# Cached keys and values of the dilation-16 heads: products on GpSimd in float32 and sums on VectorE instead of products on TensorE

## The chip, the cores and the metric

The kernel runs on one core of one Trainium2 chip. Its engines are called as the profile calls them: PE (TensorE, matrix products; its weight loads are PEld), DVE (VectorE), ACT (ScalarE), POOL (GpSimd) and SP (SyncE, which here only starts transfers). The metric is the time of one execution in microseconds (us) on the device; smaller is better.

## The reference

One inference step of a small decoder for 256 prompt tokens and 8 samples of 8 new tokens (T = 320 columns in all): a convolution layer, an MLP, an attention layer, an MLP, a norm. The change lies in the attention layer. It has 8 head slots, and each has three groups of keys: (window, dilation) = (128, 1), (512, 4), (2048, 16). For the new tokens of a sample the scores and the sums over cached keys are

```python
idx = n_past + jnp.arange(S)[:, None] - dilation * jnp.arange(n_keys)[None, :]
kg = k_cat[:, idx_c]
vg = v_cat[:, idx_c]
s = jnp.einsum('bshe,bsnhe->bhsn', q, kg, preferred_element_type=jnp.float32)
...
o = jnp.einsum('bhsn,bsnhe->bshe', p.astype(vg.dtype), vg,
               preferred_element_type=jnp.float32)
```

and the three groups are merged under one softmax. With dilation 16 and 8 new tokens no two tokens of a sample share a cached key: token s of a sample reads the 128 cached positions that are s modulo 16. So the scores of this third group are, for every token, its own 128 keys of 128 elements times its own query, and its output is its own 128 values weighted with its own row of the softmax. All inputs are float32.

## The kernel before

Every large product is done in three passes of a reduced float32 format. `load` brings 1024 KB of weights or of cached keys or values into a ring of 4 tiles `raw`; `split` makes of each half a leading part `wh` on ACT (line 122) and a rest `wl` on DVE (line 123), with rings of 4; PE then multiplies `wh` with the leading part of the other operand, `wh` with its rest, and `wl` with its leading part (lines 142 to 144, function `mm3`).

The attention layer is a list of steps that `Stream.run` writes out in PE's order, by hand: a step has a part for PE (`pe_`), a part for the other engines that comes after the next step (`post`), and possibly a half of a loaded chunk, which is split three halves ahead of its step. `qkv_steps(h)` gives the nine products of head h (36 quarters of 12 instructions on PE), `side(h)` the attention of head h; `merge` lays the side steps of head h-1 among the quarters of head h, by weights. The last head's side steps lie among `wo_steps`, the first 7 eighths of the output product; the eighth head's share (`wob`) comes behind.

For the cached part, `qk` multiplies each sample's queries, laid out as a block-diagonal operand `qpad`, with that sample's cached keys: 512 columns to an instruction, all 8 tokens of a sample against all its keys, and a mask (line 730) leaves to each token its own. Seven chunks of keys to a head, of which `k = 3..6` (four) are the dilation-16 group. `pv` does the same for 13 tiles of values, of which eight are that group's: lines 734 and 735 are the products of the keys, line 796 that of the values. POOL does nothing in this layer but start the 48 transfers that write out new keys and values (line 881), and 15 additions of the norm at its end (line 211).

Of the kernel before, what the change touches and what calls it, by code (L numbers as in the profile page):

```python
# [32 lines left out]
SEQ = 256  # L33
# [15 lines left out]
NKEY = 1664  # L49
# [21 lines left out]
B_MP = B_MS + NKEY  # L71
# [5 lines left out]
def decoder_step(ctx: ExitStack, tc: tile.TileContext, I, O):  # L77
# [38 lines left out]
    def split(raw, u0, units):  # L116
        """the units from u0 as float32r: the leading part, and the rest"""
# [39 lines left out]
    def rsqrt(out, v, after=None, temps=None):  # L157
        """out = v ** -0.5, with a Newton step"""
# [11 lines left out]
    def tokens(acc, n, eps):  # L170
        """(column sums of acc / n + eps) ** -0.5 on every partition, by way of tokens on partitions"""
# [24 lines left out]
    class Norm:  # L196
        """RMSNorm of x: its gain on the way into the next product, 1/rms on the way out"""
# [27 lines left out]
    def weave(a, b):  # L225
        """runs the steps of two lists in step with one another"""
# [10 lines left out]
    if True:  # L237
# [23 lines left out]
        with tc.tile_pool(name="conv", bufs=1) as conv:  # L261
# [27 lines left out]
            def glu_steps(f):  # L289
                """products, gate and windows of block f"""  # L290
# [49 lines left out]
            def tap_steps(fs):  # L340
                """the depthwise convolution of blocks fs: taps on VectorE (summed in PSUM), GpSimd and, for the last
                block, TensorE; then the sums for the LayerNorm"""
# [23 lines left out]
                def pool_taps(i):  # L366
                    # the share of GpSimd's taps that goes with VectorE's tap i
# [109 lines left out]
    def four(src, ps4, hi, lo, norm):  # L477
        """the products of four blocks together, along the contraction"""
# [45 lines left out]
    tmps[0].__exit__(None, None, None)  # L524
    tmp = None
    with tc.tile_pool(name="attn", bufs=1) as ap:
        oo = big.tile([128, 2, H, T], F32R, name="ah")
        oh, ol = oo[:, 0], oo[:, 1]
        zz = big.tile([128, 3 * 1024 + 13 * 128], F32R, name="al")
        qpad = zz[:, :3072].rearrange("p (g b c) -> p g b c", g=3, b=NB)  # L530
        pt = zz[:, 3072:].rearrange("p (t c) -> p t c", t=13)
        dve.tensor_scalar(zz[:, :3072].rearrange("p (a b) -> p a b", b=128),
                          ones[:, None, :].to_broadcast([128, 24, 128]), 0.0, None, op0=OP.mult)
# [10 lines left out]
        class Stream:  # L544
            """Steps in the order of TensorE's program. The weights' and caches' halves are split ahead of their step,
            and what follows a step on the other engines comes after the next step."""
# [9 lines left out]
            def run(self):  # L556
# [16 lines left out]
                for pe_, post, c, p in self.todo:  # L573
# [7 lines left out]
                    if pe_ is not None:  # L581
                        pe_()
# [6 lines left out]
        class Late:  # L589
            """a chunk that is loaded and split when told"""  # L590
# [24 lines left out]
        def side(h):  # L615
            """attention of head h: steps (quarters of a product of the next head that belong after it, step)"""
            E = {}
            L = []

            def step(w, pe_, post=None, chunk=None, part=0):  # L620
                L.append((w, (pe_, post, chunk, part)))

            def v_t(g):
# [13 lines left out]
                step(.3, go, post)  # L637

            def q_fill():
                for g in range(G):  # L640
# [4 lines left out]
            def new_s():  # L645
# [11 lines left out]
                step(.3, go, post)  # L657

            def p_s(i):
                """scores and softmax of the prompt's query block i"""  # L660
# [26 lines left out]
                step(.3, go, post)  # L687

            def p_t(i, c0):
# [7 lines left out]
                step(.3, go, post)  # L697

            def p_o(i):
# [11 lines left out]
                step(.3, go, post)  # L711

            C0 = {0: (0, 512), 2: (512, 128), 3: (640, 512), 5: (1152, 512)}

            def qk(k):
# [363 lines left out]
```

## Time and profile before

| | before |
|---|---|
| median of 3 runs | 3123.1 us (3121.42 to 3123.53) |
| span of the profiled execution | 3120.8 us |
| PE busy | 3046.0 us, 98% of the span |
| DVE busy | 1837.4 us, 59% |
| ACT busy | 1456.2 us, 47% |
| POOL busy | 253.0 us, 8% |

The table comes from one execution taken by the hardware profiler. Its span runs from the first to the last instruction; the time of a run is some 2 us longer. Busy times are those in which an engine has at least one instruction under way. PE works on several at once, so the mean of one PE instruction is longer than the distance between two of them, and the distance is what counts.

### The profile page before, as it was taken

What the parts mean: (1) busy time and instruction counts of PE and PEld (TensorE: products, weight loads), DVE (VectorE), ACT (ScalarE), POOL (GpSimd) and SP (SyncE); (2) the same over time, 40 slices, a digit from 0 to 9 for tenths busy, and PEclk for the clock granted to TensorE, in tenths of its full rate; (3) what the DMA queues carried; (4) which work ended last, traced back from release to release, by engine and by line L of the source; (5) the groups of instructions that cost most, each with busy time, mean ns of one, the idle gap of its engine ahead of it and who ended that gap; (6) DMA issues with size and microseconds to landing.
All of it is one profiled execution on the core that took longest, in us unless ns stands there. A gap on an engine that the chain in (4) does not pass through costs nothing. (4 is left out here: it accounts for less than half of the span.)

```text
span 3120.8 us, 48229 instructions
## 1 busy us (share of the span) xinstructions
PE 3046.0 (98%) x20160; PEld 2972.0 (95%) x20160; DVE 1837.4 (59%) x2360; ACT 1456.2 (47%) x2006; POOL 253.0 (8%) x261
## 2 busy tenths in 40 slices
PE   7998899999999999999999999999999999999998
PEld 6997899999999999999999999998999999999998
DVE  8998754444444444557777777778744444444444
ACT  7877644334334234435555555555532332433442
POOL 3776200000000000000000000000100000000000
PEclk9999999999999999999999999999999999999999
DMA  5443244444444444446666766676444444444442
GB/s 200 138 153 118 103 149 152 150 149 149 149 149 149 149 150 150 152 166 232 241 237 240 264 230 250 239 250 243 148 151 152 153 151 150 149 149 149 149 149 88
DMA packets 80571, 533.41 MB, mean 171 GB/s; under 512 B 11744, under 2 KB 12000, under 8 KB 19808
## 3 DMA queue, kind: packets, MB, share of 16 engines
q1 hardware_dynamic: 74304, 518.14, 47.9%
q0 software_dynamic: 2448, 8.62, 0.7%
q8 instruction: 158, 2.59, 0.3%
q10 hardware_dynamic: 3600, 3.57, 0.3%
q14 instruction: 61, 0.50, 0.0%
HBM read 517.59 MB, written 12.70 MB: 170 GB/s over the span
## 5 line engine op out<-in xcount | busy, mean ns | idle before, releaser
L123 DVE TENSOR_TENSOR wl<-raw,wh 128x1024 fp32r<-128x1024 f32 (+1 forms) x978 | 1200.9, 1236 | 826.4 <-ACT wh L122 825.4
L122 ACT ACTIVATE wh<-raw 128x1024 fp32r<-128x1024 f32 (+1 forms) x978 | 1019.8, 1055 | 1422.0 <-PE mm L143 1196.5
L142 PE MATMUL mm<-bh,wh 128*128 128x320 f32 x3200 | 990.6, 310 | 10.0 <-ACT wh L122 9.2
L143 PE MATMUL mm<-bl,wh 128*128 128x320 f32 x3200 | 986.1, 308 | 0.8 <-DVE bl L153 0.8
L144 PE MATMUL mm<-bh,wl 128*128 128x320 f32 x3200 | 985.3, 308 | 1.2 <-DVE wl L123 1.2
L142 PE MATMUL mm<-ah,wh 128*128 128x320 f32 x2896 | 895.8, 310 | 29.7 <-ACT wh L122 12.9
L144 PE MATMUL mm<-ah,wl 128*128 128x320 f32 x2896 | 894.0, 309 | 0.1
L143 PE MATMUL mm<-al,wh 128*128 128x320 f32 x2768 | 854.9, 309 | 8.2 <-DVE al L153 4.2
L142 PEld LDWEIGHTS mm<-bh,wh 128*128 128x128 f32 x3200 | 600.7, 188 | 17.4 <-ACT wh L122 9.2
L143 PEld LDWEIGHTS mm<-bl,wh 128*128 128x128 f32 x3200 | 600.8, 188 | 8.9 <-DVE bl L153 2.3
L144 PEld LDWEIGHTS mm<-bh,wl 128*128 128x128 f32 x3200 | 600.5, 188 | 2.0 <-DVE wl L123 2.0
L142 PEld LDWEIGHTS mm<-ah,wh 128*128 128x128 f32 x2896 | 544.5, 188 | 36.6 <-ACT wh L122 15.0
L144 PEld LDWEIGHTS mm<-ah,wl 128*128 128x128 f32 x2896 | 544.7, 188 | 1.2 <-DVE wl L123 0.3
L143 PEld LDWEIGHTS mm<-al,wh 128*128 128x128 f32 x2768 | 520.5, 188 | 11.2 <-DVE al L153 5.5
L374 POOL TENSOR_TENSOR pacc<-pacc,prod 128x320 f32<-128x320 f32 x168 | 180.8, 1111 | 75.5 <-ACT prod L373 74.6
L510 DVE TENSOR_TENSOR x<-x,mm 128x320 f32<-128x320 f32 x128 | 62.4, 488 | 177.4 <-PE mm L144 177.4
L505 DVE SCALAR_TENSOR_TENSOR sg<-mm,r 128x320 f32<-128x320 f32 x126 | 61.8, 492 | 162.4 <-PE mm L144 162.1
L384 DVE SCALAR_TENSOR_TENSOR s<-bl,wdw,s 128x320 f32<-128x320 f32 x272 | 130.0, 545 | 0.1
L373 ACT ACTIVATE prod<-bl,wdw 128x320 f32<-128x320 f32 x168 | 91.0, 577 | 27.7 <-POOL pacc L374 27.3
L734 PE MATMUL s<-wh,al 128*128 128x512 f32 (+1 forms) x256 | 96.1, 387 | 0.0
L735 PE MATMUL s<-wl,al 128*128 128x512 f32 (+1 forms) x256 | 90.8, 366 | 0.0
L535 POOL DMA_DIRECT2D cb<-cb x1 | 0.7, 712 | 1011.8 <-DVE acc L211 1011.8
(191 smaller groups left out, 1608.5 us busy)
## 6 DMA issues: line engine op xcount, KB each, us to landing
raw<-w SPq DMA_DIRECT2D x252, 1024.0 KB, 5.0
raw<-qkv SPq DMA_DIRECT2D x72, 1024.0 KB, 5.2
raw<-k SPq DMA_DIRECT2D x48, 1024.0 KB, 5.4
raw<-v SPq DMA_DIRECT2D x48, 1024.0 KB, 5.5
raw<-pw SPq DMA_DIRECT2D x32, 1024.0 KB, 5.1
raw<-pw2b SPq DMA_DIRECT2D x12, 1024.0 KB, 4.9
raw<-woa SPq DMA_DIRECT2D x8, 896.0 KB, 4.9
raw<-pw2a SPq DMA_DIRECT2D x4, 1024.0 KB, 4.9
```

The costliest lines, as they stand in the source:

```text
L122: act.activation(wh[:, :n], r, AF.Copy)
L123: dve.tensor_sub(wl[:, :n], r, wh[:, :n])
L142: pe.matmul(ps, wh, xh, start=start, stop=False)
L143: pe.matmul(ps, wh, xl, start=False, stop=False)
L144: pe.matmul(ps, wl, xh, start=False, stop=stop)
L373: act.activation(seg(pr_), win(f, k), AF.Copy, scale=dw(f, k))
L374: pool.tensor_add(pa, pa, pr_)
L384: dve.scalar_tensor_tensor(a, win(f, k), dw(f, k), a, op0=OP.mult, op1=OP.add)
L505: dve.scalar_tensor_tensor(t, ps, 0.0, norm.r, op0=OP.max, op1=OP.mult)
L510: dve.tensor_add(x[:, ob], x[:, ob], ps)
L734: pe.matmul(ps[:, :n], qpad[:, g, b0 + j], wh[:, j * n:j * n + n], start=False, stop=False)
L735: pe.matmul(ps[:, :n], qpad[:, g, b0 + j], wl[:, j * n:j * n + n], start=False, stop=(done and j == nb - 1))
```

## The change

The 32 products of keys and the 32 of values that belong to the dilation-16 group leave PE, in each head, and so do the splits of their 8 chunks, the mask's two products and the rows of the mask. In their place each head has 16 pieces, 8 of keys and 8 of values, one to a sample (`piece`): SP loads 512 KB, in which every token's own 128 keys (or values) stand by themselves; POOL spreads one row of 1024 numbers (the sample's 8 queries, or its 8 rows of the softmax) over all 128 partitions into the fifth part of a tile `spread`, and multiplies the piece with it; DVE sums over each 128 numbers. The rows come by small transfers of SP (`row`) from a transposed copy of the query, or from the softmax's result `S`. The sums of the keys are transposed on PE into `S` (`scores2_in`); those of the values are added to the head's output at its end (`s_end`).

The steps now have positions, in quarters of a product (36 to a head), and are sorted by them. The query of this group is made first (`QKV_ORDER`). Steps without a part for PE are written out at once. The transfers that write out new keys and values move from POOL's queue to SP's.

```diff
-NKEY = 1664
+QKV_ORDER = ((0, 2), (2, 0), (2, 1), (2, 2), (1, 0), (1, 1), (1, 2), (0, 0), (0, 1))
+NKEY = 768
+NPE = 640
...
+        spread = big.tile([128, 5, 1024], F32, name="al")
...
-                    if pe_ is not None:
-                        pe_()
+                    if pe_ is None:
+                        post()
+                        continue
+                    pe_()
...
+        def piece(kind, h, b, at):
+            n = slots[0]
+            slots[0] += 1
+            t = spread[:, n % 4]
+
+            def fetch():
+                sp.dma_start(t, I[kind + "2"][h, b])
+
+            def mult():
+                wide = spread[:, 4]
+                pool.partition_broadcast(wide, E2[kind, h, b // 4][32 * (b % 4):32 * (b % 4) + 1, :])
+                pool.tensor_mul(t, t, wide)
+
+            def total():
+                if b == 0:
+                    E2["sum", kind, h] = ap.tile([128, NB * NS], F32, name="t" + kind, bufs=2)
+                dve.tensor_reduce(E2["sum", kind, h][:, 8 * b:8 * b + 8], t.rearrange("p (a c) -> p a c", a=8),
+                                  axis=AX.X, op=OP.add)
+
+            add(at - 2.9, None, fetch)
+            add(at, None, mult)
+            add(at + 4, None, total)
+
+        def row(kind, h, half, src):
+            r = E2[kind, h, half] = ap.tile([128, 1024], F32, name="R", bufs=2)
+            for j in range(4):
+                b = 4 * half + j
+                sp.dma_start(r[32 * j:32 * j + 1, :], src[8 * b:8 * b + 8, :])
+
+        def scores2(h, t0):
...
+            add(t0 + 6, go, post)
+            for b in range(NB):
+                piece("k", h, b, t0 + 8.2 + 1.75 * b)
...
-                c = Late(I["k0"][h], 8) if k == 2 else Late(I["k1"][h, k] if k < 2 else I["k2"][h, k - 3])
+                c = Late(I["k0"][h], 8) if k == 2 else Late(I["k1"][h, k])
...
-                    E["v", t // 2] = Late(I["v"][h, t // 2]) if t < 12 else Late(I["v6"][h], 8)
+                    E["v", t // 2] = Late(I["v"][h, t // 2]) if t < 4 else Late(I["v0"][h], 8)
...
+            t2 = 12.2 if last else 22.4
+            for b in range(NB):
+                piece("v", h, b, t0 + t2 + (2 if last else 1.75) * b)
...
-                            pool.dma_start(O["kv"][h, r - 1, g], t)
+                            sp.dma_start(O["kv"][h, r - 1, g], t)
```

How this stands in the built programs, engine by engine. POOL's rows, in the middle of the attention layer of the kernel before (out_kv is the output tensor of new keys and values; in brackets what the instruction waits for):

```order
L881 DMA out_kv<-k_14736 128x320 [waits DMASW1_49,DVE_49]
L881 DMA out_kv<-k_14853 128x320 [waits DMASW2_49,DVE_49]
L881 DMA out_kv<-v_15271 128x320 [waits DMASW3_49,DVE_49]
L881 DMA out_kv<-v_15413 128x320 [waits DMASW4_49,DVE_49]
L881 DMA out_kv<-v_15531 128x320 [waits DMASW5_49,DVE_49]
```

And POOL's rows of two pieces of the changed kernel (al is the tile `spread`, R the tile of rows; an ISA row with an output is the spreading of a row, an ISA row without operands names the library of GpSimd code that the next instruction needs):

```order
L641 ISA
L641 ISA al<-R 128x1024 [waits DMAHW2_49,Pool_49]
L642 ISA
L642 TENSOR_TENSOR al<-al 128x1024 [waits DMAHW6_49,DVE_49,Pool_49]
L641 ISA
L641 ISA al<-R 128x1024 [waits Pool_49]
L642 ISA
L642 TENSOR_TENSOR al<-al 128x1024 [waits DMAHW7_49,DVE_49,Pool_49]
```

The rows without operands name library 1 ahead of the spreading and library 0 ahead of the product, in turn, so each piece holds two of them: 256 in the attention layer, which holds none before. The kernel before has one such row in all, ahead of its first product on POOL (line 280), and it names library 0.

DVE's rows in the kernel before, around the reduction of a head's output (wl is the rest of a split half):

```order
L878 SCALAR_TENSOR_TENSOR q_14951<-mm,r 128x320
L123 TENSOR_TENSOR wl<-raw,wh 128x1024 x7
L878 SCALAR_TENSOR_TENSOR q_15056<-mm,r 128x320
L123 TENSOR_TENSOR wl<-raw,wh 128x1024
L803 TENSOR_TENSOR Sp<-o,cst 128x1024
L805 TENSOR_REDUCE orr<-Sp 128x128
```

and in the changed kernel among the pieces of a head (tk and tv are the sums of keys and of values, line 647):

```order
L125 TENSOR_TENSOR wl<-raw,wh 128x1024 x2
L647 TENSOR_REDUCE tv<-al 128x8
L125 TENSOR_TENSOR wl<-raw,wh 128x1024
L946 TENSOR_TENSOR k_14009<-mm,r 128x320
L869 TENSOR_TENSOR Sp<-o,cst 128x1024
L871 TENSOR_REDUCE orr<-Sp 128x128
L647 TENSOR_REDUCE tv<-al 128x8 x2
L125 TENSOR_TENSOR wl<-raw,wh 128x1024
```

A sum stands between the splits that PE needs next, about one to every two splits, and each sum waits for POOL's product of its piece; what stands behind it on DVE waits with it.

## Rows read from the trace of the kernel before

**Rows 1.** The page, part 1: busy time, share and instructions of each engine.

```profile
PE 3046.0 (98%) x20160; PEld 2972.0 (95%) x20160; DVE 1837.4 (59%) x2360; ACT 1456.2 (47%) x2006; POOL 253.0 (8%) x261
```

**Rows 2.** Windows of the attention layer: length, busy by engine, granted clock, DMA, GB/s.

```profile
1343.20:1406.50 63.30, 63.30 (x433) 63.13 (x432) 31.53 (x35) 19.95 (x22) 3.97 (x7) 1.00 0.49 162
1406.50:2101.50 695.00, 691.63 (x4420) 648.88 (x4418) 510.54 (x625) 382.32 (x508) 22.77 (x42) 1.00 0.68 243
2101.50:2190.00 88.50, 85.52 (x534) 78.15 (x533) 71.34 (x96) 50.89 (x70) 0.00 (x0) 1.00 0.69 248
2190.00:2210.40 20.40, 17.60 (x104) 14.98 (x103) 20.25 (x33) 17.29 (x36) 15.26 (x15) 1.00 0.17 67
```

**Rows 3.** Waits, 1380 to 2250 us: total us, times, longest.

```profile
DVE wl L123 <- ACT wh L122: 170.8, 187, 2.3
```

**Rows 4.** Timeline of PE: the first side step after head 0 and head 7.

```profile
1406.36 0.38 PE L630 MATMUL s<-cst,v 128*128 128x128 f32 x2
...
2100.24 0.44 PE L630 MATMUL s<-cst,v 128*128 128x128 f32 x2
```

**Rows 5.** Timeline of PE: products with 512 columns, the first and last of seven.

```profile
2121.71 0.39 PE L735 MATMUL s<-wl,al 128*128 128x512 f32 x1
...
2123.10 0.40 PE L735 MATMUL s<-wl,al 128*128 128x512 f32 x1
```

**Rows 6.** Groups by form, 1343.2 to 2210.4 us: busy us, mean ns, idle before.

```profile
L123 DVE TENSOR_TENSOR wl<-raw,wh 128x1024 fp32r<-128x1024 f32 x362 | 435.5, 1222 | 168.5 <-ACT wh L122 167.6
...
L734 PE MATMUL s<-wh,al 128*128 128x512 f32 x192 | 81.1, 423 | 0.0
...
L796 PE MATMUL o<-wh,al 128*128 128x512 f32 x208 | 65.5, 396 | 0.0
...
L685 DVE TENSOR_REDUCE mx<-Sp 128x1 f32<-128x768 f32 x8 | 7.6, 954 | 0.3
...
L685 DVE TENSOR_REDUCE mx<-Sp 128x1 f32<-128x384 f32 x8 | 4.4, 553 | 0.3
```

**Rows 7.** Timeline of POOL: products of 320 columns, one alone and 22 without a gap.

```profile
57.38 0.87 POOL L374 TENSOR_TENSOR pacc<-pacc,prod 128x320 f32<-128x320 f32 x1 [11.15 <-ACT prod L373]
62.74 23.58 POOL L374 TENSOR_TENSOR pacc<-pacc,prod 128x320 f32<-128x320 f32 x22 [4.49 <-ACT prod L373]
```

**Rows 8.** Groups of POOL by form, whole span.

```profile
L957 POOL TENSOR_TENSOR bh<-bh,r 128x640 f32<-128x640 f32 x2 | 4.2, 2138 | 899.8 <-ACT r L954 899.8
...
L93 POOL MEMSET ones<- 128x128 f32 x1 | 0.2, 205 | 0.3 <-POOLq L1062 0.3
...
L1062 POOL MEMSET const-float32-0.0<- 128x1 f32 x1 | 0.1, 100 | 0.2 <-issue 0.2
```

**Rows 9.** Transfers: queue, count, KB each, median us from issue to landing.

```profile
raw<-w1a SPq DMA_DIRECT2D x4, 1024.0 KB, 7.7
out_kv<-v POOLq DMA_DIRECT2D x24, 160.0 KB, 5.1
out_kv<-k POOLq DMA_DIRECT2D x24, 160.0 KB, 4.5
...
cb<-cb POOLq DMA_DIRECT2D x1, 736.0 KB, 6.2
out_cp<-gl ACTq DMA_DIRECT2D x16, 15.0 KB, 1.5
```

**Rows 10.** Timeline of POOL around the kernel's one library row (line 280).

```profile
0.74 0.20 POOL L93 MEMSET ones<- 128x128 f32 x1 [0.29 <-POOLq L1062]
31.75 2.64 POOL L280 TENSOR_TENSOR pacc<-x,r 128x320 f32<-128x320 f32 x2 [30.81 <-ACT r L276]
```

**Rows 11.** Groups by form, 60 to 260 us (convolution, POOL at work).

```profile
L374 POOL TENSOR_TENSOR pacc<-pacc,prod 128x320 f32<-128x320 f32 x137 | 148.4, 1121 | 53.8 <-ACT prod L373 53.7
...
L123 DVE TENSOR_TENSOR wl<-raw,wh 128x1024 fp32r<-128x1024 f32 x49 | 71.5, 1461 | 1.6 <-ACT wh L122 1.6
```

**Rows 12.** Groups by form, 400 to 600 us (MLP, POOL idle).

```profile
L123 DVE TENSOR_TENSOR wl<-raw,wh 128x1024 fp32r<-128x1024 f32 x57 | 69.8, 1225 | 61.7 <-ACT wh L122 61.6
```

More of the change, by code (lines that the diff above doesn't have):

```diff
@@ L613, in softmax_tail, with add, go, post @@
             dve.tensor_scalar(S, S, l[:rows], None, op0=OP.mult)
-        def side(h):
+        todo = []
+        def add(pos, pe_, post=None, chunk=None, part=0):
+            todo.append((pos, len(todo), (pe_, post, chunk, part)))
+        E2 = {}
+        slots = [0]
+        def piece(kind, h, b, at):
[22 more added lines that the diff above has]
+        def scores2(h, t0):
+            def go():
+                E2["qT", h] = ps = s_tile()
+                pe.transpose(ps[:64, :128], B[h, 0, 2][:, SEQ:], ident)
+            def post():
+                q = ap.tile([64, 128], F32, name="qT")
+                act.activation(q, E2["qT", h][:64, :128], AF.Copy)
+                for half in range(2):
+                    row("k", h, half, q)
+            add(t0 + 6, go, post)
+            for b in range(NB):
+                piece("k", h, b, t0 + 8.2 + 1.75 * b)
+        def side(h, t0):
             E = {}
[L618 to L623, printed above, removed]
+            def step(pos, pe_, post=None, chunk=None, part=0):
+                add(t0 + pos, pe_, post, chunk, part)
+            def v_t(pos, g):
                 def go():
@@ L636, in post @@
                     act.activation(vn[:64, g, 2], ps[:64, 256:384], AF.Copy)
-                step(.3, go, post)
+                step(pos, go, post)
             def q_fill():
-                for g in range(G):
+                for g in range(2):
                     q = B[h, 0, g][:, SEQ:].rearrange("p (b s) -> p b s", b=NB)
@@ L853, in side, with s_end @@
-            s_out()
-            step(0, None, None)
-            return L
+                    E["os"] = ap.tile([128, 64], F32, name="os")
+                    dve.tensor_copy(E["os"], E["so"][:, :64])
+                    if last:
+                        s_end()
+                step(pos, go, post)
+            def s_end():
+                dve.tensor_add(E["os"], E["os"], E2["sum", "v", h])
+                split_in(oh[:, h, SEQ:], ol[:, h, SEQ:], E["os"])
+            last = h == H - 1
+            for g in range(G):
+                v_t(.3 * g, g)
@@ new lines, in side @@
+            step(.9, None, q_fill)
+            new_s(1)
+            scores2_in(1.3)
+            p_s(1.6, 0)
+            qk(0, 2.5, 3.5)
+            qk(1, 4.6, 5.6)
+            p_t(5, 0, 0)
+            qk(2, 6.6)
+            p_o(7.2, 0)
+            p_s(8.2, 1)
+            step(8.8, None, s_soft)
+            p_t(12.3, 1, 0)
+            p_t(12.6, 1, 3)
+            s_t(13, 0, 5)
+            n_t(13.3)
+            p_o(15.5, 1)
+            t2 = 12.2 if last else 22.4
+            step(t2 - 3, None, lambda: row("v", h, 0, E["S"][:, NPE:NKEY]))
@@ L857, in qkv_steps @@
+            step(t2 - 3 if last else t2 - .5, None, lambda: row("v", h, 1, E["S"][:, NPE:NKEY]))
+            for b in range(NB):
+                piece("v", h, b, t0 + t2 + (2 if last else 1.75) * b)
+            for t in range(5):
+                pv(17 + 2.2 * t, t)
+            step(28, None, s_red)
+            s_out(31.5)
+            if not last:
+                step(38.8, None, s_end)
         def qkv_steps(h):
@@ L907, in wo_steps @@
             return L
[L909 to L920 removed]
         norm2 = Norm(V_MLP[1])
         with tc.manual_schedule():
+            for h in range(H + 1):
+                for i, st in enumerate(qkv_steps(h) if h < H else wo_steps()):
+                    add(36 * h + (i if h < H else 1 if i == 0 else 3.5 + .92 * (i - 1)), *st)
+                if h < H:
+                    scores2(h, 36 * h)
+                if h:
+                    side(h - 1, 36 * h)
             S = Stream()
[L926 to L928 removed]
+            for _, _, st in sorted(todo, key=lambda e: e[:2]):
+                S.add(*st)
             S.run()
```

148 lines of the change are left out of this document (50 added, 98 removed).

## The prediction

> **What bounds it now.** The page's first part says PE: busy for 98% of the span, POOL for 8% [rows 1]. The windows of the attention layer say the same of this stage: it runs from 1343.2 to 2210.4 us, 867.2 us, and in its long part PE is busy for 691.63 of 695.00 us at granted clock 1.00, 2.4 GHz, DVE for 510.54 [rows 2]. The waits agree: the longest kind in total is DVE's for ACT's half of a split, and none of these is over 2.3 us [rows 3]. So time that leaves PE here is time saved, as long as the engine that takes the work over keeps up. From the first side step after head 0 to that after head 7 lie 693.88 us [rows 4], 99.1 us to a head.
>
> **What is removed.** Seven products of 512 columns start 1.39 us from first to last, six distances of 0.232 us [rows 5]. The change takes away 66 of them in each head (32 of keys, 32 of values, 2 of the mask), 15.3 us, and eight small transpositions against two new ones, which I count as nothing. The groups bear the counts out: of 192 products with `wh` on line 734 two thirds are this group's, of 208 on line 796 eight thirteenths [rows 6]. Over 8 heads 122 us, and a head would last 83.8 us. The 128 splits that vanish give DVE 128 times 1.222 us = 156 us back [rows 6], and ACT its share, which is hidden either way.
>
> **What DVE gets.** 128 sums over 1024 numbers. Reductions over 768 and 384 took 954 and 553 ns [rows 6], 1.04 ns a column, so 1.22 us: 156 us again. DVE was at 510.54 / 7 = 73 us a head [rows 2] and stays at some 70, as the softmax of the new tokens gets shorter: below 83.8. As work that is nothing; as a wait it is not, since each sum stands in DVE's queue ahead of splits that PE needs, and waits for POOL. Splits run three halves ahead of PE, so a sum that is late by more than a few quarters stops PE. If POOL falls behind, it sets the pace of all engines.
>
> **What POOL gets.** A piece is: name library 1, spread a row, name library 0, multiply. Each price by itself:
> - The product of 1024 columns. 22 products of 320 took 23.58 us, 3.35 ns a column, one alone 0.87 us, 2.7 [rows 7]; with 640 columns 2138 ns, 3.34 [rows 8]. Bounds 2.8 and 3.4 us; I take 3.4, by the row nearest in size.
> - The spreading. No row shows it. Writing 128 columns took 205 ns and one column 100 [rows 8], so 0.83 ns a column and 0.95 us for 1024 is the lower bound; a product, 3.4 us, the upper. It has one input and is nearer to the first: 1.2 us.
> - The change of library. The kernel before has one, and the row behind it says nothing: POOL sat for 30.81 us ahead of it for ACT [rows 10]. Lower bound: nothing, if it only sets an index. If it fetches code from memory, a transfer lies in it: 1.5 us at the least (15 KB out), 4.5 to 5.1 for what POOL sends out, 6.2 for the one read that POOL started, 7.7 for the slowest kind [rows 9]. I take 6.2, the only row of the same kind (POOL starts it, memory is read, POOL needs the result). That it is named anew ahead of every instruction speaks for a fetch: two libraries don't lie ready side by side.
>
> The Trainium skill (GPSIMD Engine Reference, section Instruction dispatch) says that the first call of a freshly loaded library pays a load of about 6 us (5.95 measured) which shows as no instruction. No row here shows one; by that figure alone a piece would last 16.5 us and the sum below end at about 4420 us, an estimate.
>
> A piece so lasts 6.2 + 1.2 + 6.2 + 3.4 = 17.0 us, and 16 to a head 272 us against PE's 83.8. Without the library rows it would be 4.6, 73.6 to a head, and POOL would just fit. The spare 10.2 us over 32 changes of library are 0.32 us each: from there on POOL is the bound. That is the point on which the sign hangs.
>
> **The other edits.** Loaded bytes stay the same (16 times 512 KB for 8 times 1024 KB to a head). The 48 outgoing transfers move past SP's queue, each waiting for DVE's new key or value, with loads of `raw` and of pieces behind it; `raw` is four chunks ahead and a chunk lasts PE 7 us, so this is hidden, and where POOL paces, SP has time in plenty. The rows' transfers (16 small ones to a head) are issued several quarters ahead of their piece, but for the first keys of a head: these wait for the query's product, its transposition and a transfer of at least 1.5 us, some 8 us. The library change ahead of the piece waits for no semaphore and lies in that gap, so I count 1.5 us of it a head.
>
> **The sum.** The stage starts where it did. Head 0's query, product and transposition: 17 us (13.7 to the first product's end, as the norm's factor comes with it, then PE, ACT and a transfer; an estimate). 128 pieces of 17.0: 2176, less 6 for the first change of library. Gaps of 8 heads: 12. Behind the last product a sum, the last split and the eighth head's share of the output: 2190.0 to 2210.4 took 20.4 [rows 2], so 25. Together 2224 us instead of 867.2: 1357 more. Span 3120.8 + 1357 = 4478, and the runs lie some 2 us above the span (median 3123.1): **4480 us**. PE would then be busy for about two thirds of the span, and idle two thirds of the stage.
>
> **Rivals.**
> - The change of library costs next to nothing, under 0.32 us. The schedule then closes: PE bounds, 3123 - 122 = 3001 us, some 20 less or more with the end. For it: the rows that name a library have no operand and wait for no transfer, and nothing in the trace shows a load: the first product behind the one row there starts as soon as its input is there [rows 10]. Against it: that row had 30 us to be ready in, and the reason for a fetch above. Chance 0.27. This is the case on the other side.
> - The change is free, but POOL and DVE hinder each other. Beside a busy POOL a split took 1461 ns [rows 11], with POOL idle 1225 [rows 12]: 0.24 us more, beside products of 1.07 us. With products of 3.4 us that is 0.75 us to each of 28 splits, 21 us a head; DVE at 70 + 21 = 91 us then bounds, 7 us above 83.8, and the time is 3001 + 57 = 3058 us. If splits and all of POOL's work exclude each other, a head takes 28 x 1.22 + 73.6 = 107.8 us, 8.7 above today's, and the time is 3193 us. The Trainium skill (SBUF, section Who interferes with whom) has such a rule: a DVE instruction with two inputs in SBUF and a POOL instruction that reads there exclude each other for a whole instruction; the 1461 ns agree in sign with it. Chance 0.10, half of it below 3123.
> - The change of library costs, but less: only one of two in a piece is exposed, or a fetch takes 1.5 to 3 us. One of two: a piece of 10.8 us, 128 of them 1382, the stage about 1436, 3692 us. At 1.5 us each a piece of 7.6, the stage 1025, 3281 us. Chance 0.17, 3281 to 4000.
> - The forecast: both exposed, 4.5 to 7.7 us each: 4045 to 4860 us. Chance 0.46; its own range with the middle rows of the transfers, 4.5 to 6.8, is 4045 to 4630.
>
> **Chances.** Faster by over 0.2% (about 6 us, what a measurement here can tell): 0.27 + 0.05 = 0.32. Slower: 0.46 + 0.17 + 0.03 = 0.66. The same: 0.02. The range must hold cases of both signs: from the cheap rival, 2995, to 4630, which leaves out some 0.15, mostly above.
>
> **What would show it.** If right: POOL's products stand 17 us apart through the stage, with the gap not accounted for by the two instructions; the longest waits are DVE's sums (line 647) for POOL's products, then PE for DVE's splits; the chain of waits names POOL; the stage runs from 1343 to about 3567. If the products stand about 4.6 us apart and PE stays near 98%, the first rival holds. Splits of 2 us and more beside products would show the second, a gap ahead of only one of the two instructions the third. The forecast is wrong if two libraries can lie ready, or if POOL fetches the next while it works on the last.

## The result and the profile after

The changed kernel takes 4592.7 us (median of 4 runs, 4585.57 to 4596.66) beside 3123.3 us (3121.42 to 3124.28): a ratio of 1.470, interval 1.468 to 1.4721. The forecast was 4480. The profiled execution has a span of 4594.7 us, 1473.9 more than before.

The page of the changed kernel, the lines that answer to [rows 1] and three of the 40 slices (tenths of busy time; PEclk is the granted clock):

```profile
PE 3147.3 (68%) x19584; PEld 3063.3 (67%) x19584; DVE 1802.0 (39%) x2304; ACT 1316.3 (29%) x1862; POOL 696.7 (15%) x469
...
PE   8989999999993644325443254432434399999998
...
POOL 4660000000002121221212212122121200000000
PEclk9999999999996767657666576666767699999999
```

Outside the attention layer little has changed (4594.7 - 2346.8 = 2247.9 us by the windows below, where it was 3120.8 - 867.2 = 2253.6). Within it, PE stands at 2 to 6 tenths and POOL, which now sets the pace, at 1 or 2. Here is the trap of this profile: the engine that paces the stage is busy for a fifth of it. The windows, which answer to [rows 2] (length, busy by engine, granted clock, DMA share, GB/s):

```profile
1343.20:1406.50 63.30, 43.13 (x277) 42.22 (x275) 20.05 (x22) 14.27 (x16) 10.44 (x6) 0.87 0.37 133
1406.50:3560.00 2153.50, 864.19 (x4401) 806.35 (x4401) 531.22 (x645) 290.50 (x427) 437.43 (x239) 0.67 0.24 86
3560.00:3665.00 105.00, 33.94 (x141) 31.72 (x142) 28.79 (x34) 9.97 (x12) 22.28 (x12) 0.61 0.23 84
3665.00:3690.00 25.00, 22.86 (x143) 21.44 (x143) 24.04 (x36) 18.78 (x37) 15.40 (x15) 0.97 0.14 48
```

The stage now runs from 1343.2 to about 3690 us, 2346.8 us where it was 867.2 (I read its end to some 5 us). PE is busy for 964 of them. No engine is busy for half of the long window, so some engine waits for something that isn't work. The waits of the whole span, which answer to [rows 3] (total us, times, longest):

```profile
ACT wh L124 <- PE mm L145: 2072.1, 599, 22.4
...
POOL al L642 <- issue: 925.3, 126, 11.7
...
DVE tk L647 <- POOL al L642: 847.9, 64, 17.8
DVE tv L647 <- POOL al L642: 809.0, 63, 15.7
DVE wl L125 <- ACT wh L124: 702.2, 572, 4.1
PEld mm L146 <- DVE wl L125: 628.9, 52, 19.1
PE mm L146 <- DVE wl L125: 614.2, 51, 18.8
POOL al L641 <- issue: 604.8, 101, 8.3
```

Read them from the end of the chain: ACT waits for PE, since its rings are full; PE waits for DVE's rest of a split, up to 18.8 us, where its longest wait for one in the kernel before was 0.6 (1380 to 2250 us); DVE stands in its sums and waits for POOL; and POOL waits for "issue", which means for nothing that the profile can name. POOL's own timeline of two and a half pieces (start, length, idle time before it in brackets) shows where this time lies:

```profile
2004.95 1.31 POOL L641 PARTITION_BROADCAST al<-R  x1 [5.91 <-issue]
2013.02 2.33 POOL L642 TENSOR_TENSOR al<-al 128x1024 f32<-128x1024 f32 x1 [6.76 <-issue]
2021.36 1.30 POOL L641 PARTITION_BROADCAST al<-R  x1 [6.02 <-issue]
2029.80 2.33 POOL L642 TENSOR_TENSOR al<-al 128x1024 f32<-128x1024 f32 x1 [7.14 <-issue]
2038.18 1.30 POOL L641 PARTITION_BROADCAST al<-R  x1 [6.05 <-issue]
```

Ahead of each instruction POOL idles for 6 or 7 us: 5.9 (median of 128) ahead of a spreading, 7.0 ahead of a product. A piece is 5.9 + 1.3 + 7.0 + 2.3 = 16.6 us (16.62 is the median distance of two products), and the forecast had 17.0. The groups by form give the two works their sizes:

```profile
L642 POOL TENSOR_TENSOR al<-al 128x1024 f32<-128x1024 f32 x128 | 299.0, 2336 | 938.9 <-issue 925.3 <-DMA raw<-qkv 6.9 <-DVE wl L125 6.7
...
L641 POOL PARTITION_BROADCAST al<-R x128 | 170.3, 1330 | 903.0 <-issue 604.8 <-DMA R<-qT 109.5 <-DMA R<-S 58.0
```

469 us of work stand against 1842 us of idle time. From one head's first spreading to the next one's (1815.29 and 2100.53 us) lie 285.2 us, where a head lasted 99.1 [rows 4]: 16 pieces of 16.6 and one gap, at the border of two heads. The timeline of all engines across such a border:

```profile
1794.31 2.33 POOL L642 TENSOR_TENSOR al<-al 128x1024 f32<-128x1024 f32 x1 [6.97 <-issue]
1796.68 1.22 DVE L647 TENSOR_REDUCE tv<-al 128x8 f32<-128x1024 f32 x1 [8.39 <-POOL al L642]
...
1799.42 1.22 DVE L125 TENSOR_TENSOR wl<-raw,wh 128x1024 fp32r<-128x1024 f32 x1 [0.72 <-ACT wh L124]
...
1800.57 0.48 DVE L944 SCALAR_TENSOR_TENSOR q<-mm,r 128x320 f32<-128x320 f32 x1
...
1805.35 0.41 PE L665 MATMUL s<-cst,q 128*64 128x128 f32 x1
...
1808.71 0.25 ACT L669 ACTIVATE qT<-s 64x128 f32<-64x128 f32 x1
...
1815.29 1.30 POOL L641 PARTITION_BROADCAST al<-R  x1 [18.65 <-DMA R<-qT]
1826.67 2.37 POOL L642 TENSOR_TENSOR al<-al 128x1024 f32<-128x1024 f32 x1 [10.08 <-issue]
```

The next head's query (line 944) stands in DVE's queue behind the last sum of the head before, and that sum waits for POOL. So the query, its transposition, its copy and its rows' transfer begin only when POOL has finished: 18.65 us, in which the change of library ahead of the spreading (5.9 us) is hidden. Behind the border the change back costs more than the usual 7.0 us, here 10.08.

### The profile page after: what moved, and what is told of

It is laid out like the page before. It is cut to its first block, busy times and chain, and to the rows that moved or that the text cites. A ratio compares the mean times of both kernels' runs of the same rounds, so it can differ in the third digit from the quotient of the medians.

```text
span 4594.7 us, 47887 instructions
## 1 busy us (share of the span) xinstructions
PE 3147.3 (68%) x19584; PEld 3063.3 (67%) x19584; DVE 1802.0 (39%) x2304; ACT 1316.3 (29%) x1862; POOL 696.7 (15%) x469
## 2 busy tenths in 40 slices
DMA packets 96381, 533.65 MB, mean 116 GB/s; under 512 B 13793, under 2 KB 21217, under 8 KB 43809
## 5 line engine op out<-in xcount | busy, mean ns | idle before, releaser
L124 ACT ACTIVATE wh<-raw 128x1024 fp32r<-128x1024 f32 (+1 forms) x850 | 892.1, 1055 | 2418.2 <-PE mm L145 2072.1
L146 PE MATMUL mm<-bh,wl 128*128 128x320 f32 x3200 | 1058.7, 331 | 597.8 <-DVE wl L125 597.8
L125 DVE TENSOR_TENSOR wl<-raw,wh 128x1024 fp32r<-128x1024 f32 (+1 forms) x850 | 1051.3, 1242 | 703.3 <-ACT wh L124 702.2
L144 PE MATMUL mm<-bh,wh 128*128 128x320 f32 x3200 | 1059.3, 331 | 10.7 <-ACT wh L124 9.2
L145 PE MATMUL mm<-bl,wh 128*128 128x320 f32 x3200 | 1048.6, 328 | 0.9 <-DVE bl L155 0.9
L144 PEld LDWEIGHTS mm<-bh,wh 128*128 128x128 f32 x3200 | 661.4, 207 | 17.1 <-ACT wh L124 9.2
L642 POOL TENSOR_TENSOR al<-al 128x1024 f32<-128x1024 f32 x128 | 299.0, 2336 | 938.9 <-issue 925.3
L647 DVE TENSOR_REDUCE tk<-al 128x8 f32<-128x1024 f32 x64 | 78.1, 1220 | 847.9 <-POOL al L642 847.9
L647 DVE TENSOR_REDUCE tv<-al 128x8 f32<-128x1024 f32 x64 | 78.1, 1220 | 809.0 <-POOL al L642 809.0
L641 POOL PARTITION_BROADCAST al<-R x128 | 170.3, 1330 | 903.0 <-issue 604.8
```

Of the source, the lines that this page charges most:

```text
L124: act.activation(wh[:, :n], r, AF.Copy)
L125: dve.tensor_sub(wl[:, :n], r, wh[:, :n])
L144: pe.matmul(ps, wh, xh, start=start, stop=False)
L145: pe.matmul(ps, wh, xl, start=False, stop=False)
L146: pe.matmul(ps, wl, xh, start=False, stop=stop)
L641: pool.partition_broadcast(wide, E2[kind, h, b // 4][32 * (b % 4):32 * (b % 4) + 1, :])
```

## The experiments

"After" is the changed kernel. Times without a range are single runs; where there are several, they lie within 8 us of their median (e5: 10), so differences of single runs are good to about 10 us. Where the edits say ..., lines of the same kind are left out (positions, buffers, the naming of the library).

**What a change of library costs.** The first two take it away.

e1_one_library. One library holds the code of both instructions; it is named once (POOL does so at 0.9 us of the span), and no change is left in the stage. Against after:

```diff
+        from concourse import library_config
+        pool.load_library(library_config.all_libraries[10])
         B = {}
```

> One library that holds both the spreading and the product is named once, ahead of the attention layer, so no library row stands in it; nothing else differs from the changed kernel. If the changes of library are the cause (each 5.9 to 7 us on POOL), POOL needs 1.3 + 2.3 = 3.6 us a piece, 58 a head, PE bounds again: 3123 - 122 = 3001 us, up to 3058 if splits and products hinder each other. If POOL's own work, its rows' transfers or SP's order were the cause, it stays above 4000 us.

Measured: 3146.2 us (3138.71 to 3147.84), ratio to the kernel before 1.0059, interval 1.0046 to 1.0073. These two lines take 1447 us away, 5.65 for each of 256 changes. But 3001 is missed by 145 us, and the kernel is 0.6% slower than before. The groups of its stage:

```profile
L125 DVE TENSOR_TENSOR wl<-raw,wh 128x1024 fp32r<-128x1024 f32 x233 | 392.3, 1698 | 35.2 <-ACT wh L124 31.5 <-PE mm L145 2.9 <-PE s L807 0.3
...
L644 POOL TENSOR_TENSOR al<-al 128x1024 f32<-128x1024 f32 x128 | 384.6, 3005 | 19.5 <-DMA al<-v 6.2 <-DMA al<-k 2.6
...
L643 POOL PARTITION_BROADCAST al<-R x128 | 210.5, 1645 | 239.0 <-DMA R<-qT 159.3 <-DVE Sp L755 40.0 <-DMA R<-S 28.4
```

Without the changes POOL and DVE are busy at the same time, and each is slower for it: the split 1698 ns for 1222 [rows 6], the product 3005 for 2336, the spreading 1645 for 1330. Its timeline shows how:

```profile
1618.79 1.30 POOL L643 PARTITION_BROADCAST al<-R  x1
1620.17 2.38 POOL L644 TENSOR_TENSOR al<-al 128x1024 f32<-128x1024 f32 x1
...
1665.25 2.15 POOL L643 PARTITION_BROADCAST al<-R  x1
1667.49 3.28 POOL L644 TENSOR_TENSOR al<-al 128x1024 f32<-128x1024 f32 x1
...
1672.25 3.17 POOL L644 TENSOR_TENSOR al<-al 128x1024 f32<-128x1024 f32 x1
...
1673.48 3.02 DVE L125 TENSOR_TENSOR wl<-raw,wh 128x1024 fp32r<-128x1024 f32 x1
```

A spreading lasts either 1.30 or 2.15 us; most products lie near 2.38 or between 3.0 and 3.35, and a split beside one goes from 1.22 to between 2.1 and 3.4. The split shown begins during a product and ends, at 1676.50, 1.08 us after that product's end at 1675.42. That looks like waiting for a whole instruction of the other engine, or for most of one, not like a shared rate. The sums, with one input, stay at 1.21 us. The window of seven heads, between the first side steps of heads 0 and 7 (columns as above):

```profile
1415.70:2118.60 702.90, 624.09 (x3903) 588.77 (x3902) 569.45 (x568) 257.32 (x382) 509.71 (x219) 0.95 0.65 240
```

e2_named_again. Is it the naming that costs, or the change? e1, with the same library named anew ahead of every product:

```diff
                 pool.partition_broadcast(wide, E2[kind, h, b // 4][32 * (b % 4):32 * (b % 4) + 1, :])
+                pool.load_library(both)
                 pool.tensor_mul(t, t, wide)
```

> As e1, but the same library is named again ahead of every product (128 rows, none of which changes anything). If only a change costs, the time of e1, about 3000 to 3060 us. If every naming fetches anew, a piece lasts 6.5 + 1.3 + 2.3 = 10.1 us, 128 of them 1293, with the gaps between heads of the changed kernel (170 us) and its ends a stage of some 1510 us: about 3770 us.

Measured: 3142.2 us, within the runs of e1. Naming a library that is already there costs nothing that this run can tell; the change costs.

e3_before_unused. Does a change disturb anything but POOL? The kernel before, with 32 tiny pairs (8 columns) whose result nobody uses, so 64 changes:

```diff
+                        if q == 1 and j % 2:
+                            pool.partition_broadcast(idle[:, :8], idle[0:1, 8:])
+                            pool.tensor_mul(idle[:, :8], idle[:, :8], idle[:, 8:])
```

> The kernel before, with 32 pairs of a spreading and a product of 8 columns on POOL in the attention layer, on a tile of their own that nobody reads: 64 changes of library by themselves, with nothing waiting for them. If a change costs 5.9 to 7 us wherever it stands, POOL idles that long ahead of each of the 64 instructions, some 13 us a pair, and the time stays within 10 us of 3123, since nobody waits. If the idle time in the changed kernel came from its waits, the gaps here are under 1 us.

Measured: 3124.5 us, beside 3125.9 for the kernel before on the same chip. POOL's timeline:

```profile
1413.63 0.28 POOL L870 PARTITION_BROADCAST idle<-idle  x1 [6.62 <-issue]
1421.08 0.61 POOL L871 TENSOR_TENSOR idle<-idle 128x8 f32<-128x8 f32 x1 [7.17 <-issue]
```

The change is there (6.62 and 7.17 us in these rows, 9.2 and 7.9 on the mean, 5.7 to 12.1 in all), and the time stays. So these 64 changes held up POOL and nothing else. Why some last longer, no run shows.

e4_pairs. After, with pieces two at a time (two spreadings, then two products): half the changes, the same work.

```diff
+                if b % 2 == 0:
+                    held.append((t, E2[kind, h, b // 4], b))
+                    return
+                pair = (held.pop(), (t, E2[kind, h, b // 4], b))
+                for i, (t_, r_, b_) in enumerate(pair):
+                    pool.partition_broadcast(spread[:, 3 + i], r_[32 * (b_ % 4):32 * (b_ % 4) + 1, :])
+                for i, (t_, r_, b_) in enumerate(pair):
+                    pool.tensor_mul(t_, t_, spread[:, 3 + i])
...
-            add(at + 4, None, total)
+            add(at + 2.3, None, total)
```

> The changed kernel with its pieces taken two at a time: two rows spread, then two products (three piece buffers in place of four, two for rows, and the sum 2.3 quarters behind in place of 4): 128 changes of library instead of 256, the same work otherwise. If the changes are the cause, two pieces last 6 + 2.6 + 7 + 4.7 = 20.3 us, 10.1 each: 128 of them 1293 us in place of 2125, about 3770 us. If POOL's own work or the transfers are the cause, about 4590 us or more, as a buffer is missing.

Measured: 3850.2 us. POOL's timeline:

```profile
2000.17 2.48 POOL L646 PARTITION_BROADCAST al<-R  x2 [7.17 <-issue]
2009.83 4.63 POOL L648 TENSOR_TENSOR al<-al 128x1024 f32<-128x1024 f32 x2 [7.18 <-issue]
```

With 256, 128 and no changes the time is 4593, 3850 and 3146 us: the first 128 changes taken away save 5.8 us each, the others 5.5. That is nearly a straight line, and it leaves no room for another cause of that size.

**Where PE's 122 us went.** With the changes gone, the kernel should have been at 3001.

e11_no_pieces. e1 without the pieces: no loads, spreadings, products and sums of this group (the sums are set to zero by ACT):

```diff
-            add(at - 2.9, None, fetch)
-            add(at, None, mult)
-            add(at + 4, None, total)
+            if b == 0:
+                def blank():
+                    E2["sum", kind, h] = ap.tile([128, NB * NS], F32, name="t" + kind, bufs=2)
+                    act.activation(E2["sum", kind, h], x[:, 0, :NB * NS], AF.Copy, scale=0.0)
+                add(at + 4, None, blank)
```

> e1 without pieces: no loads, spreadings, products and sums of the group (its sums are zero, so the group's scores and sums are left out); all else as in the changed kernel. It is what PE, splits and positions alone need. By the count of products on PE 3123 - 122 = 3001 us, within 10; if the new positions cost PE something of their own, more.

Measured: 3000.7 us. In the window of seven heads PE is never idle:

```profile
1414.20:1991.90 577.70, 577.70 (x3904) 558.79 (x3902) 349.79 (x461) 258.70 (x393) 0.00 (x0) 1.00 0.54 191
```

PE's part of the change is worth 122 us, as worked out; the pieces take it back. This window is the measure for the others, since PE has the same 3902 to 3904 instructions in it: in e1 they take 702.9 us instead of 577.7, of which 78.8 are idle time of PE and 46.4 are longer busy time, at a granted clock of 0.95 instead of 1.00. All of the idle time is put down to waits for DVE's results, 29.6 us to the reduction of a head's output, 25.9 to splits, 17.3 to the query, but for 2.3 us for ACT.

e7_no_spread. e1 without the spreadings: the products take one constant row, which is left in place.

```diff
+        pool.memset(spread[:, 4], 1.0)
...
-                pool.partition_broadcast(wide, E2[kind, h, b // 4][32 * (b % 4):32 * (b % 4) + 1, :])
```

> e1 with the spreading left out (the products take a constant row, so the scores and sums of the group are not the reference's); positions of the changed kernel. A piece is then one product, 2.33 us alone. If POOL's load and the ports set e1's time, 16 x 3.1 + 23 = 73 us a head lies under PE's 83.8, and the time is about 3001 to 3035 us. If the sums' place in DVE's queue or SP's order set it, it stays near 3146.

Measured: 3065.4 us, a miss of 30 us and more. Loads, products and sums alone cost 65 us over e11. The split is at 1599 ns, the product at 2851. Seven heads:

```profile
1413.50:2038.20 624.70, 595.31 (x3904) 567.92 (x3902) 552.14 (x569) 257.05 (x382) 311.87 (x111) 0.98 0.73 270
```

PE is idle for 29.4 us and busy for 17.6 more than in e11. So taking away the spreadings, with the wait for their rows, takes away 81 of e1's 145 us, and the rest costs 65.

e12_before_products. Does mutual exclusion alone cost time? The kernel before, with 32 products of 512 columns a head on POOL, which nobody waits for and which need no change:

```diff
+                        if q % 2 and j < 8:
+                            for _ in range(2):
+                                pool.tensor_mul(idle, idle, idle)
```

> The kernel before with 32 unused products of 512 columns on POOL to each head, about 38 us a head, no library change, nobody waiting: only POOL's reading beside DVE's splits. If they exclude each other, splits (1222 ns in the kernel before) last 1.5 to 1.8 us in this layer, but 44 x 1.22 + 38 = 92 us a head still fits into 99.1, so the time stays within 15 us of 3123. If they don't, splits stay at 1.22 us.

Measured: 3149.7 us beside 3124.9, 25 us more in one run, where I had expected at most 15. Its groups:

```profile
L123 DVE TENSOR_TENSOR wl<-raw,wh 128x1024 fp32r<-128x1024 f32 x359 | 538.1, 1533 | 79.4 <-ACT wh L122 77.9
...
L871 POOL TENSOR_TENSOR idle<-idle 128x512 f32<-128x512 f32 x256 | 419.1, 1637 | 17.3
```

Splits of 1533 ns instead of 1222 [rows 6], and nothing of this kernel waits for these products. The outgoing transfers, which stand in POOL's queue behind them, are the other thing that this edit delays; but no engine's wait in the stage names them. PE's waits in it total 23 us (9 in the kernel before), nearly all for DVE's results: 11.9 for the reduction of a head's output (3.3), 4.7 for the softmax (0.7), 2.0 for splits (0.6). So the trace speaks for the hindrance as the cause, and not for the transfers; these waits account for some 14 of the 25 us, and the rest stays open.

e5_even. In e1 POOL waits 159.3 us for the next head's rows, seven times, longest 24.8. The pieces lie 1.75 quarters apart and leave the time between heads empty. Here e1 with its pieces 2.1 quarters apart and the values' beginning later:

```diff
-                piece("k", h, b, t0 + 8.2 + 1.75 * b)
+                piece("k", h, b, t0 + 8.2 + (2.1 if h < H - 1 else 1.75) * b)
...
-            t2 = 12.2 if last else 22.4
+            t2, dt = (12.2, 2) if last else (22.4, 1.75) if h == H - 2 else (25, 2.1)
...
```

> e1 (one library, 3146 us) with the pieces laid evenly: 2.1 quarters apart in place of 1.75, values from 25 in place of 22.4, for all heads but the last two. In e1 POOL waits some 23 us a head for the row of the next head's query. If that wait, which the positions set, is what keeps the head at 100.4 us, the wait falls to about 6 us and a head to 16 x 5.0 + 6 = 86 us: about 3030 to 3050 us. If splits on DVE and POOL's work exclude each other, a head can't be shorter than 28 x 1.22 + 16 x 3.63 = 92 us, and the time is about 3070 to 3090. If neither, it stays at 3146.

Measured: 3117.3 us (11 runs, 3111.83 to 3126.87), ratio 0.9975, interval 0.9966 to 0.9985. That is 29 us less than e1 and the only version with all of the work in it that lies below the kernel before, by 0.25%, about as much as can be told. Neither expectation is reached. POOL still waits 149.1 us for rows, and the splits are at 1815 ns. Seven heads:

```profile
1412.30:2090.60 678.30, 620.87 (x3903) 589.14 (x3902) 615.36 (x568) 257.19 (x382) 506.64 (x219) 0.95 0.67 249
```

PE's idle time falls from 78.8 to 57.4 us and its busy time by 3: that is the gain on e1. DVE is now busy for 91% of the window, where e11 has 61%. The 109 sums in it are 132 of the 266 us that it has more than in e11; nearly all of the rest is splits that last longer (194 in the window, 1884 ns on the mean where e11 has 1222).

e9_even_early. e5 with the query transposed at quarter 4.3 and the pieces from 6.5, 2.2 apart:

```diff
-            add(t0 + 6, go, post)
+            add(t0 + 4.3, go, post)
...
-                piece("k", h, b, t0 + 8.2 + 1.75 * b)
+                piece("k", h, b, t0 + 6.5 + (2.2 if h < H - 1 else 1.85) * b)
...
```

> e5 (3117 us; 96.9 us a head, of which POOL waits 17 for the row of the next query) with that query transposed 1.7 quarters earlier, its pieces from 6.5 in place of 8.2, and all pieces 2.2 quarters apart. If POOL's wait for the row is what is left of the loss, it shrinks to some 6 us and a head lasts about 88 us: 3050 us. If exclusion of splits and POOL's work bounds (92 us a head and more), about 3080 to 3095.

Measured: 3140.7 us (ratio 1.0051, interval 1.0038 to 1.0063), a miss: slower than e5. POOL's wait for rows falls to 107.0 us. Seven heads, and what PE waits for in them:

```profile
1419.60:2118.20 698.60, 620.78 (x3902) 590.01 (x3900) 625.27 (x569) 256.38 (x382) 515.66 (x220) 0.94 0.67 242
```

```profile
PE s L878 <- DVE orr L873: 27.6, 7, 4.1
PE s L667 <- DVE q L946: 21.7, 6, 4.4
PE s L766 <- DVE Sp L620: 20.7, 7, 4.7
```

PE's busy time is that of e5; the 20 us of difference are idle time, 77.8 for 57.4. The transposition (line 667), put earlier, now stands in PE's queue waiting for the query, 21.7 us, which in e5 it doesn't (there the query is waited for with 5.7 us, on line 712). So the earlier transposition moved a wait from POOL, which had slack, to PE, which has none; the other spacing moved further waits of PE up and down (27.6 us instead of 15.3 for the reduction of the output, none instead of 14.7 for the splits ahead of line 808).

e8_mixed. e5 with every other product on DVE:

```diff
-                pool.tensor_mul(t, t, wide)
+                if n % 2:
+                    pool.tensor_mul(t, t, wide)
...
+                if n % 2 == 0:
+                    dve.tensor_mul(t, t, wide)
...
```

> e5 with every other product on DVE (1.22 us in place of 2.33 on POOL), three piece buffers, two for rows, sums 2.3 quarters behind. Splits, spreadings and products that exclude each other: 34.2 + 16 x 1.3 + 8 x 2.33 + 8 x 1.22 = 83.4 us a head, DVE busy 70 + 10 = 80: about 3020 to 3060 us. If only POOL's queue bounds, 16 x 1.3 + 8 x 2.33 = 39 us a head, 3001 us. If DVE is the bound with its waits, 3090 or more.

Measured: 3145.1 us (ratio 1.0073, interval 1.0059 to 1.0086), a miss. The splits get shorter, 1472 ns, but 64 products of 1971 ns lie on DVE, and it is busy for 619.45 of 680 us, where e5 had 615.54. Only three buffers are left for pieces, so loads come later too: POOL's waits for them are 153.7 us.

**Spreading by a transfer instead.** If POOL didn't spread, no change would be needed and one of POOL's instructions would be gone. Both runs have three buffers for pieces in place of four.

e6_dma_spread. e5, with SP spreading the row by a transfer that reads one partition 128 times:

```diff
+                sp.dma_start(wide, bass.AP(tensor=r.tensor, offset=r.offset, ap=[list(r.ap[0]), [0, 128], [1, 1024]]))
...
```

> The rows are spread by transfers of SP in place of POOL (512 KB to a piece from one partition's row; three piece buffers, two for rows, the even positions): POOL has only products, library 0, and no change of library anywhere. POOL and splits then need 28 x 1.22 + 16 x 2.33 = 71.5 us a head, under the 83.8 of PE: about 3001 to 3040 us if the transfers keep up. They move 32 MB a head, 380 GB/s at 84 us; if that is the bound, or a transfer from one row is slow, about 3100 us or more.

Measured: 4930.3 us (ratio 1.5779, interval 1.5758 to 1.5801), slower than the changed kernel itself. The waits from 1343 to 3690 us and a row of POOL's timeline:

```profile
POOL al L646 <- DMA al<-R: 2058.5, 113, 59.3
```

```profile
2040.45 2.34 POOL L646 TENSOR_TENSOR al<-al 128x1024 f32<-128x1024 f32 x1 [17.47 <-DMA al<-R]
```

In the 680 us from 1410 on, the DMA engines are busy for 0.90 of the time and move 105 GB/s.

e10_dram_spread. The same with the rows in memory (a transfer out, then one into all 128 partitions), and the query transposed at quarter 4.3:

```diff
+            r = E2[kind, h, half] = rows_.tile([4, 1024], F32, name="R", bufs=4)
+            sp.dma_start(r.rearrange("a (b c) -> (a b) c", c=128), src[32 * half:32 * half + 32, :])
...
+                sp.dma_start(wide, bass.AP(tensor=r.tensor, offset=r.offset, ap=[[0, 128], [1, 1024]]))
...
```

> No spreading on POOL and no library change: SP writes the rows to memory and reads each back into 128 partitions, 512 KB to a piece; three piece buffers, two for rows, even positions, early query. If e6 was slow (4930 us, 20 us a piece) since one partition's row was read 128 times, and not since 32 MB a head are too much, this runs near e7 or below: 3010 to 3065 us. If it is the amount, 3100 us or more.

Measured: 3223.6 us (ratio 1.0312, interval 1.0298 to 1.0326). In the windows the queues carry nearly three times as much:

```profile
1410.00:2090.00 680.00, 562.72 (x3409) 536.07 (x3408) 481.21 (x495) 223.90 (x327) 237.03 (x93) 0.89 0.78 287
```

With another source of the rows 1707 us are gone. The positions, which differ too, moved the time by 20 to 30 us elsewhere (e5, e9), so the one-partition source was the cause of nearly all of that. But POOL waits 474.6 us for rows even so, 92 times up to 2230 us, and the version is slower than e1's spreading.

## Why the prediction was right

Its side and its mechanism held: two changes of library to a piece, both exposed, set POOL's pace, and POOL sets that of all engines. Its size came near in part by luck, as errors of both signs met in it. By its steps:

- **What bounds, and what is removed.** 122 us by six distances of 0.232 us: e11 gives 3000.65 where 3001 was worked out.
- **The change of library, 6.2 us.** Measured: 5.9 ahead of the spreading (5.7 to 6.1 as a rule), 7.0 ahead of the product; 12.9 a piece for 12.4. Both are exposed, but for the one ahead of a spreading that waits for its rows. The row of a transfer from memory that POOL started came near in size; that such a transfer lies in a change is not shown: the profile of after lists 96381 packets of DMA and that of e1, without the 256 changes, 96376. The Trainium skill (GPSIMD Engine Reference, section Instruction dispatch) has 5.95 us for the first call of a freshly loaded library; the trace agrees ahead of the spreading, and ahead of the product it is a microsecond more. The page speaks of a first call; with two libraries in turn every call is one.
- **The product, 3.4 us.** 2.34. Even the lower bound, 2.8, was too high. The 3.35 ns a column, read from the 22 products without a gap [rows 7], held the hindrance of the second rival already: five of them last 1.85 to 1.97 us, the other seventeen 0.88 on the mean, as the one alone. Of all 168 products on line 374, 38 last 1.84 us and more, and every one of them has one of DVE's splits running at its start or within 0.04 us of it. What is left scales with a fixed share: 8 columns take 0.20 us (e3), 320 take 0.88, 1024 take 2.33, some 0.2 us and 2.1 ns a column (an estimate from these three).
- **The spreading, 1.2 us.** 1.33 on the mean, 1.30 at the median.
- **The sum on DVE, 1.22 us.** 1.220.
- **The gaps, 1.5 us a head, 12 in all: the step that was mis-sized.** Measured: 127 distances of products take 2286.3 us, and 127 times the median of 16.62 is 2110.7, so 175.5 lie in gaps. Eight long ones hold 152 of them: the first is head 0's values, which wait for its softmax (POOL idle 40.46 us), and seven are borders of heads. I had put 8 us from query to rows and let the change hide 6 of them. At the borders POOL idles 18.65 to 23.09 us, because the query itself waits for POOL's last piece through DVE's queue, and then for a quarter of PE's work. I had named this queue in the part on DVE and didn't carry it to the border. Over the seven borders that is 97 us beyond the usual change; another 18 lie behind them, where five of the seven changes back take 10.0 to 11.7 us instead of 7.0, and why they do stays open.
- **The sum.** From the start of the stage to the first spreading 19.3 us, from there to the end of the last product 2297.8, behind it 29.7: 2346.8. Forecast: 17, 2182 and 25. The pieces are 49 us under the forecast, the gaps 164 above (23 of the measured ones are many small delays), the lead and the end 7: 123 us in all. The rest of the span is 6 us shorter than before, and the median lies 2 us below this span, where I had added 2. That is the 4593 for 4480. The 49 us are errors that partly cancel: products 136 us too long over 128 pieces, changes 68 too short, spreadings 13 too short, some 6 between the instructions. With the product's own 2.33 us and all else the same, the forecast would have been about 4344.
- **What would show it.** The order of the waits came as said, DVE's sums for POOL and PE for DVE's splits; the products lie 16.6 us apart; PE is busy for 68% of the span (and idle for 59% of the stage, where I had two thirds); the stage ends some 123 us behind the 3567 that I gave. One thing I had wrong: the chain of waits names POOL for 0.3% and "issue" for 1.3% of the span, as it covers only a short stretch before the end; the waits and POOL's timeline had to tell it.

Of the rivals, the free change of library falls by e1 and e4; one exposed change out of two falls by POOL's timeline, and so does a cheap change of 1.5 to 3 us. Yet both prices of the second rival, 3058 with hindered splits and 3193 with full exclusion, lie around what came out once the changes were gone: 3146. The Trainium skill (SBUF — State Buffer, section Who interferes with whom) says that DVE instructions with two inputs in SBUF and POOL instructions that read SBUF exclude each other; e1's lengths, which fall into groups, agree, the sums with one input (1.21 us) stay out of it, and the spreading counts as such a reader (1.30 or 2.15 us).

The point on which I hung the sign, 0.32 us a change, was too generous: with no change at all, e1 is still slower than before. The piece itself came out as I had it, 4.65 us beside a busy DVE for 4.6. But its places leave POOL 1.75 quarters, and with a quarter of 83.8 / 36 = 2.33 us these are 4.07. I had compared whole heads, where the gaps between the two spans of pieces are POOL's to use; the schedule doesn't let it. That is only a part of e1's loss: e5, which spreads the pieces, gains 29 of the 145 us, and e7, whose pieces of 2.85 us fit into their places, still loses 65.

So the 122 us went to waits for DVE, to which nearly all of PE's idle time is put down in e1, e5, e7 and e9. DVE feeds PE, it got sums in its queue that wait for POOL, and its splits got longer beside POOL's work; PE then waits, and in the stretches with these waits its granted clock is 0.94 to 0.98 instead of 1.00. What stays open is the split between the two causes in e5's 117 us over e11: e7 (65 us without spreadings) and e12 (25 us with hindrance and no waiting) only bound it.

## What to carry to other kernels

Before two kinds of GpSimd instructions go into one loop, look which library each needs: in turn they cost 6 to 7 us for every switch here, up to 12, which no row of busy time shows; put them in one library that holds both (here two lines, 1447 us), or do many of a kind before switching. Work moved from TensorE to GpSimd isn't free even where GpSimd is idle: with two-input VectorE work beside it both get longer, by 0.3 to 0.7 us an instruction on the mean here, and if VectorE feeds TensorE the gain goes back that way. And where a slow engine's result is read by an in-order queue that also carries the next round's first step, count the whole start-up of a round as exposed.

## What the hardware showed beside that

- A library change is invisible as an instruction. The instructions of line 641 and of POOL's sequencer (a count, shortest, median and longest ns, and the time of the first and last):

```profile
L641 POOLq MODIFY_POOL_CONFIG  x256: 1/1/37, 1349.1 to 3644.0; - x128
L641 POOL PARTITION_BROADCAST al<-R x128: 1302/1302/2354, 1362.5 to 3649.8; - x128
```

  Each naming shows as two records. It takes 1 to 37 ns ahead of a spreading and 129 ns ahead of a product (line 642); the 6 or 7 us are idle time behind it.
- With rows spread by transfers from one SBUF partition into 128 (512 KB written each), POOL waited 18.2 us for each on the mean, with DMA engines that show as 0.90 busy and move 105 GB/s in all (e6); with the rows read from memory they moved 287 GB/s in all at 0.78 (e10).
- PE's granted clock was 0.67 in the long window for 1.00 before [rows 2], between its two levels of 1.2 and 2.4 GHz. Across the border of heads shown above, products of 320 columns are 0.27 us apart at first (12 from 1802.15 to 1805.08 us) and 0.15 apart from 1807.86 on. In this stretch of the border that costs some 1.4 us of the 18.65; PE had waited 7.00 us before it (to 1799.44). Elsewhere in the stage PE waits for what hangs on POOL anyway.
